# Opening of a two-layer encoder: two tiles turned by products with a diagonal of their roots, later tiles loaded into idle rows, and the last residual tile into a weight slot

## The chip, the cores and the metric

The kernel runs on one core of a Trainium2 chip. The metric is the device time of one execution in microseconds (us); lower is better. The core has a matrix engine (PE, with its weight loads PEld), a vector engine (DVE), a scalar engine (ACT), a general engine (POOL) and a queue engine (SP) that issues most transfers. Each engine takes its instructions in order; semaphores tie them together.

## The reference

Two groups of tokens (256 and 512) go through a trunk of width 1024 with two layers. Cut to what matters here:

```python
def rms_norm(x, g):
    return x * rsqrt(mean(x * x, axis=-1) + 1e-6) * g

for i in range(2):
    h = rms_norm(x, norm_mix_pre[i])
    m = window_gqa_sink(h, ...) if i == 0 else diff_attention(h, ...)   # each: qkv = h @ w_in, softmax, o @ w_o
    x = x + rms_norm(m, norm_mix_post[i])
    h = rms_norm(x, norm_ffn_pre[i])
    x = x + rms_norm(swiglu(h, w_gate_up, w_down), norm_ffn_post[i])
```

All is float32, and the products have to be nearly that exact.

## The kernel before

The 768 tokens are six tiles `t` of 128 rows. A tile is normalised row by row, turned (128 columns of it at a time, so that features lie on partitions) and split into a rounded high part `hhi` and a rest `hlo` (`split`, L364 on ACT and L365 on DVE); weights are split in the same way into `whi` and `wlo` (`two_parts`, L273 and L274). Each product of float32 accuracy is then three products `hi*hi`, `hi*lo`, `lo*hi` (L376 to L378).

The opening is what lies ahead of the first attention: for each tile, `scaled(row_rstd(x))` makes `y_pre` (square and row sum on ACT L427, plus epsilon on ACT L420, power -1/2 on POOL L421, times root and norm weight `gpre` on DVE L431); `transposes` turns it by eight PE transposes into two PSUM banks `tp_h` and splits each bank in one piece of 512 columns per engine. The key and value product of a tile, `pkva` (24 products, from four weight pieces `wa[0..3]`, two blocks `k` of 128 features each), needs all eight blocks of the tile. `a_fill` lists the order of the products: `pkva` of tiles 0, 1, 2, then the query product `pqa` of the first half, then `pkva` 3, 4, 5. `enter` and `entered` normalise tile `t + 2` while tile `t` is being multiplied. The order of the instructions on each engine is chosen by a scheduler within the constraints `issue_after`.

A tile `x` lies in one of two slots of the pool `xpool`; raw weights lie in two slots `wraw`. At the end of the second layer the down projection writes rows `y[t]` (`yf` in the profile); `finish` and `last_tile` add the residual tile `x`, which is read back from DRAM (`xd`), and store the sum (`ys`). The last residual tile, of tile 5, is loaded by `begin(5)` into an `xpool` slot, the one that tile 3 holds before. The rows `o[t]` (six tiles of 128x1024, name `oa`) take the attention output of the first layer; nothing is written to them in the opening.

Of the kernel before, what the change touches and what calls it, by code (L numbers as in the profile page):

```python
# [9 lines left out]
F32 = mybir.dt.float32  # L10
F32R = mybir.dt.float32r
BF16 = mybir.dt.bfloat16
AF = mybir.ActivationFunctionType
# [4 lines left out]
P = 128  # L18
# [70 lines left out]
def trunk(  # L89
# [18 lines left out]
    rope_b,  # L108
    yp,
# [166 lines left out]
    def prepare(upto):  # L276

        while state["split"] < min(upto, len(units), state["cap"] or len(units)):
# [35 lines left out]
            with ExitStack() as after:  # L314
                if state["after"] is not None:
                    after.enter_context(tc.issue_after(state["after"].ins))
                if 4 <= i < 8:
                    after.enter_context(tc.issue_after(state["rstd"].ins))
                    after.enter_context(tc.issue_after(state["scaled"].ins))
                if 4 <= i < N_PLAIN_A:  # L320
                    nc.gpsimd.dma_start(out=hi[:, :n], in_=raw_src[r][0])
                    state["raw_lo"] = nc.vector.tensor_tensor(
                        out=lo[:, :n], in0=src[:, :n], in1=hi[:, :n].bitcast(F32), op=ALU.subtract)
                else:
                    two_parts(hi[:, :n], lo[:, :n], src[:, :n])
# [365 lines left out]
    def mixer_a(gains, first_steps, o):  # L691
        with ExitStack() as st:
# [25 lines left out]
            def straight(i, t):  # L718
# [6 lines left out]
                def end():  # L725
# [5 lines left out]
                    rope(t1, t2, kr, pm[:, 256:].rearrange("p (n d) -> p n d", d=HD), 2, t)  # L731
# [412 lines left out]
    def ffn(layer, later, comb, cpool, cstack, ostack, gains):  # L1144
# [193 lines left out]
        with ExitStack() as st:  # L1338
# [144 lines left out]
            if not final:  # L1483
# [84 lines left out]
    head = ctx.enter_context(ExitStack())  # L1568
    first = head.enter_context(tc.tile_pool(name="first", bufs=1))
    xs_sb = [load_x(0, 0)]  # L1570
    g_in = gain(g_pre[0], "gpre", "0")
    fetch(2)
    xs_sb.append(load_x(0, 1))
    fetch(4)
    xs_sb.append(load_x(0, 2))
    small_inputs()
    xs_sb.append(load_x(0, 3))
    y_in = {}

    def enter(t):  # L1580
        x = xs_sb[t]
        y_in[t] = new_y(f"pre0_{t}")
        scaled(y_in[t], x, row_rstd(x, y_in[t], f"pre0_{t}"), g_in)

    def entered(t):
# [8 lines left out]
    enter(0)  # L1594
    with tc.issue_after(state["rstd"].ins), tc.issue_after(state["scaled"].ins):
        prepare(2)
    for s in transposes(y_in.pop(0), 0, "h0_0"):
        s()
    with tc.issue_after(state["hi"].ins), tc.issue_after(state["lo"].ins):
        enter(1)  # L1600
    with tc.issue_after(state["scaled"].ins), tc.issue_after(state["rstd"].ins):
        prepare(4)
    head.close()
    with tc.issue_after(state["raw_hi"].ins), tc.issue_after(state["raw_lo"].ins):
        small_tables()
        enter(2)
    ready = {t - 1: [lambda t=t: entered(t)] for t in range(1, NT)}

# [4 lines left out]

    def gains(i):
# [3 lines left out]
    o, ostack = rows("oa")  # L1618
# [8 lines left out]
def _layout(inp):  # L1627
# [51 lines left out]
    out["rope_b"] = c(np.stack([np.tile(rows(np.concatenate(p, axis=1)), (2, 1)) for p in ((cs, cs), (-sn, sn))]))  # L1679
    return out  # L1680
# [21 lines left out]
```

## Time and profile before

| | |
|---|---|
| time, median of 3 runs (lowest to highest) | 1643.13 us (1639.62 to 1646.32) |
| the profiled execution: its time, its span | 1638.01 us, 1636.2 us |
| PE busy in the span | 1607.4 us (98%) |
| DVE, ACT, POOL busy | 1201.5 us (73%), 942.5 us (58%), 169.3 us (10%) |
| first PE instruction | 8.04 us after the start |
| moved by DMA | 233.07 MB, mean 142 GB/s |

The profiled execution is the slowest core's own recording: its span runs from the first to the last instruction, and its time holds 1.8 us around it. Its time is 0.3% under the median of the runs. A busy share near 100% on PE means that a stage is bound there; where PE is idle, the row of its next instruction names what ended the wait.

### The profile page before, as it was taken

What the parts mean: (1) busy time and instruction counts of PE and PEld (TensorE: products, weight loads), DVE (VectorE), ACT (ScalarE), POOL (GpSimd) and SP (SyncE); (2) the same over time, 40 slices, a digit from 0 to 9 for tenths busy, and PEclk for the clock granted to TensorE, in tenths of its full rate; (3) what the DMA queues carried; (4) which work ended last, traced back from release to release, by engine and by line L of the source; (5) the groups of instructions that cost most, each with busy time, mean ns of one, the idle gap of its engine ahead of it and who ended that gap; (6) DMA issues with size and microseconds to landing.
All of it is one profiled execution on the core that took longest, in us unless ns stands there. A gap on an engine that the chain in (4) does not pass through costs nothing. (4 is left out here: it accounts for less than half of the span.)

```text
span 1636.2 us, 24435 instructions
## 1 busy us (share of the span) xinstructions
PE 1607.4 (98%) x9055; PEld 1489.5 (91%) x9055; DVE 1201.5 (73%) x2076; ACT 942.5 (58%) x1999; POOL 169.3 (10%) x261
## 2 busy tenths in 40 slices
PE   7999999999999999999999999999999999999998
PEld 7888878999999998888999999888999999998887
DVE  6778857887667755988585886857887667656986
ACT  6589976644444444556475666766644444444553
POOL 1121001000000000001220250421000000000010
PEclk9999999999999999999999999999999999999999
DMA  6532205443433247675432332505453432337664
GB/s 214 174 99 71 95 15 177 170 170 112 145 111 117 102 143 249 225 266 189 140 109 67 98 82 80 153 1 170 164 171 125 135 117 95 127 132 249 227 244 166
DMA packets 73384, 233.07 MB, mean 142 GB/s; under 512 B 9073, under 2 KB 17457, under 8 KB 73009
## 3 DMA queue, kind: packets, MB, share of 16 engines
q1 hardware_dynamic: 55008, 178.82, 32.1%
q0 software_dynamic: 18112, 52.44, 10.6%
q8 instruction: 71, 1.16, 0.3%
q14 instruction: 49, 0.39, 0.1%
q10 hardware_dynamic: 144, 0.26, 0.0%
HBM read 171.71 MB, written 42.86 MB: 131 GB/s over the span
## 5 line engine op out<-in xcount | busy, mean ns | idle before, releaser
L274 DVE TENSOR_TENSOR wlo<-wraw,whi 128x1024 fp32r<-128x1024 f32 (+1 forms) x161 | 190.7, 1188 | 185.4 <-ACT whi L273 184.7
L273 ACT CAST whi<-wraw 128x1024 fp32r<-128x1024 f32 (+1 forms) x161 | 164.6, 1024 | 124.5 <-PE py L377 59.2
L376 PE MATMUL py<-hhi,whi 128*128 128x384 f32 x480 | 160.9, 335 | 0.7 <-ACT whi L273 0.7
L377 PE MATMUL py<-hlo,whi 128*128 128x384 f32 x480 | 160.4, 334 | 0.0
L378 PE MATMUL py<-hhi,wlo 128*128 128x384 f32 x480 | 160.0, 334 | 0.0
L364 ACT CAST hhi<-araw 128x768 fp32r<-128x768 f32 (+1 forms) x74 | 57.6, 782 | 91.9 <-DMA araw<-act 89.5
L378 PE MATMUL pv<-whi,hlo 128*128 128x512 f32 (+1 forms) x240 | 92.2, 384 | 0.4 <-DVE hlo L365 0.4
L376 PE MATMUL pv<-whi,hhi 128*128 128x512 f32 (+1 forms) x240 | 92.4, 385 | 0.0
L377 PE MATMUL pv<-wlo,hhi 128*128 128x512 f32 (+1 forms) x240 | 92.3, 384 | 0.0
L376 PEld LDWEIGHTS py<-hhi,whi 128*128 128x128 f32 x480 | 90.1, 188 | 1.9 <-ACT whi L273 1.3
L377 PEld LDWEIGHTS py<-hlo,whi 128*128 128x128 f32 x480 | 90.1, 188 | 0.0
L378 PEld LDWEIGHTS py<-hhi,wlo 128*128 128x128 f32 x480 | 90.1, 188 | 0.0
L365 DVE TENSOR_TENSOR hlo<-araw,hhi 128x768 fp32r<-128x768 f32 (+1 forms) x74 | 65.2, 888 | 33.5 <-ACT hhi L364 33.3
L1228 POOL DMA_DIRECT2D act<-st x22 | 19.3, 877 | 631.5 <-DVE st L1227 601.3
L376 PE MATMUL po<-whi,hhi 128*128 128x512 f32 x192 | 78.5, 409 | 0.0
L376 PE MATMUL px<-hhi,whi 128*128 128x384 f32 x224 | 75.6, 337 | 1.7 <-ACT sv L1171 1.7
L1025 ACT ACTIVATE be<-bsc,bmx 128x512 f32<-128x512 f32 (+1 forms) x96 | 58.7, 614 | 29.7 <-DVE bmx L1023 29.2
L377 PE MATMUL po<-wlo,hhi 128*128 128x512 f32 x192 | 75.2, 392 | 0.0
L378 PE MATMUL po<-whi,hlo 128*128 128x512 f32 x192 | 75.2, 392 | 0.0
L377 PE MATMUL px<-hlo,whi 128*128 128x384 f32 x224 | 75.0, 335 | 0.0
L378 PE MATMUL px<-hhi,wlo 128*128 128x384 f32 x224 | 74.9, 334 | 0.0
L1023 DVE TENSOR_REDUCE bmx<-bsc 128x1 f32<-128x512 f32 (+1 forms) x96 | 55.2, 593 | 11.6 <-PE bsc L1019 11.3
(318 smaller groups left out, 4915.9 us busy)
## 6 DMA issues: line engine op xcount, KB each, us to landing
wraw<-in_wgu SPq DMA_DIRECT2D x60, 512.0 KB, 4.4
act<-st POOLq DMA_DIRECT2D x22, 1344.0 KB, 6.6
araw<-act SPq DMA_DIRECT2D x70, 384.0 KB, 3.9
y_wraw<-in_wgu SPq DMA_DIRECT2D x40, 512.0 KB, 4.0
wraw<-in_wd SPq DMA_DIRECT2D x40, 512.0 KB, 3.8
xd<-x SPq DMA_DIRECT2D x18, 512.0 KB, 2.9
x<-xd SPq DMA_DIRECT2D x18, 512.0 KB, 4.3
wraw<-in_wo SPq DMA_DIRECT2D x16, 512.0 KB, 3.5
```

The costliest lines, as they stand in the source:

```text
L273: state["raw_hi"] = nc.scalar.copy(out=hi, in_=src)
L274: state["raw_lo"] = nc.vector.tensor_tensor(out=lo, in0=src, in1=hi.bitcast(F32), op=ALU.subtract)
L364: state["hi"] = nc.scalar.copy(out=hi, in_=src)
L365: state["lo"] = nc.vector.tensor_tensor(out=lo, in0=src, in1=hi.bitcast(F32), op=ALU.subtract)
L376: nc.tensor.matmul(out, ah, bh, start=start and i == 0, stop=False, skip_group_check=more)
L377: nc.tensor.matmul(out, ah, bl, start=False, stop=False, skip_group_check=more)
L378: state["mm"] = nc.tensor.matmul(out, al, bh, start=False, stop=stop and i == last, skip_group_check=more)
L1023: nc.vector.tensor_reduce(out=mx, in_=s, axis=AX.X, op=ALU.max, negate=True)
L1025: nc.scalar.activation(out=e[:, :n * P], in_=s, func=AF.Exp, bias=mx, accum_out=den[:, c:c + 1])
L1228: nc.gpsimd.dma_start(out=at_hand[c // 4][:, :, c // 2 % 2], in_=out.pop(c // 2))
```

## The change

In the opening:

- Tile 0 comes in two halves of 512 columns, each squared on its own. A small input `g_col` holds the first norm weight as a column (feature `p` of block `k` at row `p`, column `k`).
- Tiles 0 and 1 are no longer scaled on DVE. The root of each row is put on a diagonal (`diag`, identity times root), and eight float32 products `x_block^T * diag` turn and scale in one. The norm weight is then a scale per partition in the split: ACT writes `hhi = g * v`, DVE writes `hlo = g * v - hhi`, both for one block of 128 columns at a time, so eight pieces on each engine and tile instead of two. Weight pieces 0 to 3 are split between these pieces; the first in two halves.
- Tiles 2 to 5 land in the idle rows `oa` early, all six loads standing ahead of the query weights on SP; `gpre` is loaded after the first weight pieces. Tiles 2 to 5 are normalised as before, but the squares of tile `t + 2` stand behind the split of tile `t`, and the scaling of tile `t + 1` behind that of tile `t`.
- The rotation of the keys on DVE stands behind the last scaled tile.

At the end, the residual tile of tile 5 lands in a slot of the raw weights (`wraw`), and its load stands ahead of the last tiles' work.

```diff
-    xs_sb = [load_x(0, 0)]
-    g_in = gain(g_pre[0], "gpre", "0")
+    o, ostack = rows("oa")
+    x0 = xpool.tile([P, D], F32, tag="x", name="x0_0")
+    for cols in halves_of:
+        nc.sync.dma_start(out=x0[:, cols], in_=x_at[0][0][:, cols])
+    nc.sync.dma_start(out=g_at, in_=g_col)
     fetch(2)
     xs_sb.append(load_x(0, 1))
     fetch(4)
-    xs_sb.append(load_x(0, 2))
-    small_inputs()
-    xs_sb.append(load_x(0, 3))
+    g_in = gain(g_pre[0], "gpre", "0")
+    for t in range(2, NT):
+        nc.sync.dma_start(out=o[t], in_=x_at[0][t])
+        xs_sb.append(o[t])
+        if t == 2:
+            small_inputs()
...
+    def diagonal(t, r):
+        diag = early.tile([P, P], F32, tag="diag", name=f"diag{t}", bufs=1)
+        state["scaled"] = nc.vector.tensor_scalar(out=diag, in0=ident, scalar1=r, scalar2=None, op0=ALU.mult)
...
+    def turn_first(t, x, diag):
...
+                nc.tensor.matmul(tp[:, j * P:(j + 1) * P], x[:, k * P:(k + 1) * P], diag, start=True, stop=True)
...
+        def part(k):
+            v = tps[k // 4][:, k % 4 * P:k % 4 * P + P]
+            h1, l1 = htile(t, k)
+            state["hi"] = nc.scalar.activation(out=h1, in_=v, func=AF.Copy, scale=g_at[:, k:k + 1])
+            state["lo"] = nc.vector.scalar_tensor_tensor(
+                out=l1, in0=v, scalar=g_at[:, k:k + 1], in1=h1.bitcast(F32), op0=ALU.mult, op1=ALU.subtract)
...
     def entered(t):
-        for s in transposes(y_in.pop(t), t, f"h0_{t}"):
-            s()
-        if t + 2 < NT:
-            if t + 3 < NT:
-                xs_sb.append(load_x(0, t + 3))
-            with tc.issue_after(state["hi"].ins), tc.issue_after(state["lo"].ins):
-                enter(t + 2)
+        if t == 1:
+            with behind("mm"):
+                part = turn_first(1, xs_sb[1], diag_1)
+            for k in range(KT):
+                with behind("hi", "lo"):
+                    part(k)
+            squares(2)
+        else:
+            for s in transposes(y_in.pop(t), t, f"h0_{t}"):
+                s()
+        if t + 1 < NT:
+            scale_in(t + 1)
...
+        if t + 2 < NT:
+            squares(t + 2)
...
+            x_of[5] = wpool.tile([P, 1024], F32, tag="wraw", name=f"x{sub}_5", bufs=RAW["w"])
+            load(x_of[5], x_at[sub][5])
...
                 if k == 0:
                     stage(4, 1)
-                    begin(5)
```

Where it moves instructions: first ACT around tiles 1 and 2. A name's first digit is the tile, `tp_h0_1_0` is the first bank of tile 1, `va0` the copy of tile 0's values out of `pkva0`. Before:

```order
L427 ACTIVATE y_pre0_2_219,ss_pre0_2_220<-x0_2_151 128x1024 [waits DMAHW7_49]
L364 CAST hhi0_110<-tp_h0_1_0_253 128x4x128 [waits PE_49]
L420 ACTIVATE rstd_pre0_2_222<-ss_pre0_2_220,eps_sb_103 128x1 [waits Activation_49]
L364 CAST hhi0_110<-tp_h0_1_1_260 128x4x128 [waits PE_49]
L727 COPY va0_288<-pkva0_240 128x256 [waits PE_49]
```

And now:

```order
L1627 ACTIVATE hhi0_110<-tp_h0_1_0_258,g_at_149 128x128 [waits PE_49]
L1627 ACTIVATE hhi0_110<-tp_h0_1_0_258,g_at_149 128x128 [waits DVE_49]
L730 COPY va0_318<-pkva0_245 128x256 [waits PE_49]
L1627 ACTIVATE hhi0_110<-tp_h0_1_0_258,g_at_149 128x128 [waits DVE_49] x2
L1627 ACTIVATE hhi0_110<-tp_h0_1_1_263,g_at_149 128x128
L1627 ACTIVATE hhi0_110<-tp_h0_1_1_263,g_at_149 128x128 [waits DVE_49] x3
L430 ACTIVATE y_pre0_2_284,ss_pre0_2_285<-oa2_139 128x1024 [waits DMAHW1_49]
L730 COPY va1_378<-pkva1_332 128x256 [waits PE_49,Activation_49]
L423 ACTIVATE rstd_pre0_2_287<-ss_pre0_2_285,eps_sb_103 128x1 [waits Activation_49]
```

The squares of tile 2 stood ahead of tile 1's split and now stand behind all of it, and the root of tile 2 behind the copy `va1`, which waits for the last product of tile 1. Each piece of `hhi` but the first of a bank waits for DVE: the semaphore's value is that of the `hlo` piece of the block before it, so the two engines take turns within a bank. Tile 0's pieces wait in the same way, with the splits of weight pieces 1 to 3 and the squares of tile 1 between them.

Second, PE from tile 1's product to tile 2's. Before, tile 2 is turned two products into `pkva1`:

```order
L376 MATMUL pkva1_302<-whi0_168,hhi0_110 128x384 [waits Activation_49]
L377 MATMUL pkva1_302<-wlo0_169,hhi0_110 128x384
L469 MATMUL tp_h0_2_0_312<-ident_81,y_pre0_2_219 128x128 [waits DVE_49]
L469 MATMUL tp_h0_2_0_312<-ident_81,y_pre0_2_219 128x128 x3
L469 MATMUL tp_h0_2_1_319<-ident_81,y_pre0_2_219 128x128 x4
L378 MATMUL pkva1_302<-whi0_168,hlo0_112 128x384 [waits DVE_49]
```

And now after the last product of `pkva1`, and right ahead of `pkva2`, which reads it:

```order
L381 MATMUL pkva1_332<-whi3_231,hlo0_112 128x384 [waits DVE_49]
L472 MATMUL tp_h0_2_0_342<-ident_81,y_pre0_2_284 128x128 [waits DVE_49]
L472 MATMUL tp_h0_2_0_342<-ident_81,y_pre0_2_284 128x128 x3
L472 MATMUL tp_h0_2_1_349<-ident_81,y_pre0_2_284 128x128 x4
L379 MATMUL pkva2_390<-whi0_193,hhi0_110 128x384 [waits Activation_49]
L380 MATMUL pkva2_390<-wlo0_194,hhi0_110 128x384
L381 MATMUL pkva2_390<-whi0_193,hlo0_112 128x384 [waits DVE_49]
```

Between the two products PE's order now holds nothing but the transposes of tile 2.

Third, SP at the end. Before, the load of the last residual tile stands behind a store and waits for a transfer:

```order
L247 DMA x3_3_15944<-xd2_3_129 128x1024 [waits DMAHW1_49,DMAHW0_49]
L247 DMA x3_4_16023<-xd2_4_130 128x1024 [waits DMAHW4_49]
L548 DMA ys<-x3_3_15944 128x1024 [waits DVE_49]
L247 DMA x3_5_16088<-xd2_5_131 128x1024 [waits DMAHW2_49]
L548 DMA ys<-x3_4_16023 128x1024 [waits DVE_49]
```

And now ahead of both stores, with no wait:

```order
L248 DMA x3_3_15973<-xd2_3_129 128x1024 [waits DMAHW3_49,DMAHW2_49]
L248 DMA x3_4_16052<-xd2_4_130 128x1024 [waits DMAHW6_49]
L248 DMA x3_5_16098<-xd2_5_131 128x1024
L551 DMA ys<-x3_3_15973 128x1024 [waits DVE_49]
L551 DMA ys<-x3_4_16052 128x1024 [waits DVE_49]
```

From the fourth key and value product to the end of the second layer's down projection, the order on all engines is what it was.

More of the change, by code (lines that the diff above doesn't have):

```diff
@@ L108, in trunk @@
     rope_b,
+    g_col,
     yp,
@@ L324, in prepare @@
                 else:
-                    two_parts(hi[:, :n], lo[:, :n], src[:, :n])
+                    for j in range(0, n, HALF if i == 0 else n):
+                        c = slice(j, j + HALF if i == 0 else n)
+                        two_parts(hi[:, c], lo[:, c], src[:, c])
             if kind == "t14" and units[i - 2][0] == "plain":
@@ L730, in end @@
                     kr, t1, t2 = (own[:, i] for i in range(3))
-                    rope(t1, t2, kr, pm[:, 256:].rearrange("p (n d) -> p n d", d=HD), 2, t)
+                    with tc.issue_after(state["scaled"].ins):
+                        rope(t1, t2, kr, pm[:, 256:].rearrange("p (n d) -> p n d", d=HD), 2, t)
                     if t == 0:
@@ new lines, in trunk, with norm_first @@
+    fetch(2)
+    xs_sb.append(load_x(0, 1))
+    fetch(4)
+    g_in = gain(g_pre[0], "gpre", "0")
[4 more added lines that the diff above has]
+            small_inputs()
+    y_in = {}
+    def norm_first(t, x):
+        ss = small.tile([P, 2], F32, tag="sso", name=f"ss_pre0_{t}")
+        junk = new_y(f"pre0_{t}")
+        cols = halves_of if t == 0 else [slice(0, D)]
+        for j, c in enumerate(cols):
+            nc.scalar.activation(
+                out=junk[:, c], in_=x[:, c], func=AF.Square, scale=D ** -0.5, accum_out=ss[:, j:j + 1])
+            if j == 0 and t == 0:
+                nc.scalar.activation(out=ss[:, 0:1], in_=ss[:, 0:1], func=AF.Identity, bias=eps_sb[:, 0:1])
+        return rstd(ss[:, 1:2], ss[:, 0:1], f"pre0_{t}") if t == 0 else rstd(ss[:, 0:1], eps_sb[:, 0:1], f"pre0_{t}")
@@ new lines, in diagonal @@
+    def diagonal(t, r):
+        diag = early.tile([P, P], F32, tag="diag", name=f"diag{t}", bufs=1)
+        state["scaled"] = nc.vector.tensor_scalar(out=diag, in0=ident, scalar1=r, scalar2=None, op0=ALU.mult)
+        return diag
+    def turn_first(t, x, diag):
+        tps = []
+        for b in range(2):
+            tp = bank(f"tp_h0_{t}_{b}")
+            for j in range(4):
+                k = 4 * b + j
+                nc.tensor.matmul(tp[:, j * P:(j + 1) * P], x[:, k * P:(k + 1) * P], diag, start=True, stop=True)
+            tps.append(tp)
+        def part(k):
[4 more added lines that the diff above has]
+                out=l1, in0=v, scalar=g_at[:, k:k + 1], in1=h1.bitcast(F32), op0=ALU.mult, op1=ALU.subtract)
+        return part
@@ new lines, in behind, with two @@
+    def behind(*names):
+        stack = ExitStack()
+        for n in names:
+            stack.enter_context(tc.issue_after(state[n].ins))
+        return stack
+    def two(part, k):
+        for j in (k, k + 1):
+            part(j)
+    r0 = norm_first(0, x0)
+    part = turn_first(0, x0, diagonal(0, r0))
+    with behind("rstd", "scaled"):
+        prepare(1)
+    with behind("raw_hi", "raw_lo"):
+        two(part, 0)
+    with behind("hi", "lo"):
+        prepare(2)
+    with behind("raw_hi", "raw_lo"):
+        two(part, 2)
@@ new lines, in trunk, with squares @@
+    with behind("hi", "lo"):
+        prepare(3)
+    with behind("raw_hi"):
+        r1 = norm_first(1, xs_sb[1])
+    with behind("rstd", "raw_lo"):
+        two(part, 4)
+    with behind("rstd", "hi", "lo"):
+        diag_1 = diagonal(1, r1)
+        prepare(4)
+    with behind("raw_hi", "raw_lo"):
+        two(part, 6)
+    head.close()
+    rs = {}
+    def squares(t):
+        y_in[t] = new_y(f"pre0_{t}")
+        with behind("hi", "rstd"):
+            rs[t] = row_rstd(xs_sb[t], y_in[t], f"pre0_{t}")
@@ new lines, in scale_in, with entered @@
+    def scale_in(t):
+        with behind("lo"):
+            scaled(y_in[t], xs_sb[t], rs.pop(t), g_in)
+    def entered(t):
+        if t == 1:
+            with behind("mm"):
+                part = turn_first(1, xs_sb[1], diag_1)
+            for k in range(KT):
+                with behind("hi", "lo"):
+                    part(k)
[5 more added lines that the diff above has]
+            scale_in(t + 1)
+        if t == 1:
+            with behind("scaled"):
+                small_tables()
+        if t + 2 < NT:
+            squares(t + 2)
@@ L1614, in gains @@
+    ready = {t - 1: [lambda t=t: entered(t)] for t in range(1, NT)}
     def gains(i):
```

32 lines of the change are left out of this document (6 added, 26 removed).

## The prediction

> **What bounds the kernel now.** I read the busy shares first, then the stretches around the two edited places, then the instructions there in order of time.
>
> ```profile
> PE 1607.4 (98%) x9055; PEld 1489.5 (91%) x9055; DVE 1201.5 (73%) x2076; ACT 942.5 (58%) x1999; POOL 169.3 (10%) x261
> 8.00:20.00 12.00, 11.63 (x54) 10.31 (x55) 9.33 (x16) 8.84 (x18) 1.78 (x3) 1.00 1.02 373
> 20.00:48.00 28.00, 28.00 (x179) 27.65 (x178) 19.10 (x49) 15.24 (x43) 3.85 (x7) 1.00 0.30 98
> 48.00:80.00 32.00, 28.97 (x183) 27.00 (x182) 26.29 (x83) 19.96 (x63) 6.54 (x12) 1.00 0.63 209
> ```
>
> The kernel is bound by PE. In the stretches (second column the length, third PE's busy time) PE works almost without a gap from 8 to 48 us; so whatever delays PE's first work, or opens a gap before 48 us, moves everything behind it. In the opening:
>
> ```profile
> 4.13 1.06 ACT L427 ACTIVATE y_pre<-x 128x1024 f32<-128x1024 f32 x1 [1.90 <-DMA x<-in_xp]
> 5.68 0.56 POOL L421 TENSOR_TENSOR rstd_pre<-rstd_pre,mhalf 128x1 f32<-128x1 f32 x1 [3.55 <-ACT rstd_pre L420]
> 6.70 1.28 DVE L431 SCALAR_TENSOR_TENSOR y_pre<-x,rstd_pre,gpre 128x1024 f32<-128x1024 f32 x1 [4.73 <-DMA gpre<-in_g_pre]
> 7.63 0.83 ACT L273 CAST whi<-wraw 128x768 fp32r<-128x768 f32 x1 [2.03 <-DMA wraw<-in_wa]
> 8.04 1.97 PE L469 MATMUL tp_h<-ident,y_pre 128*128 128x128 f32 x8 [8.04 <-DVE y_pre L431]
> 8.50 0.96 DVE L274 TENSOR_TENSOR wlo<-wraw,whi 128x768 fp32r<-128x768 f32 x1 [0.52 <-ACT whi L273]
> 9.49 1.14 ACT L364 CAST hhi<-tp_h 128x512 fp32r<-128x512 f32 x2
> 10.12 0.69 PE L376 MATMUL pkva<-whi,hhi 128*128 128x384 f32 x1
> 10.50 1.28 DVE L365 TENSOR_TENSOR hlo<-tp_h,hhi 128x512 fp32r<-128x512 f32 x2
> 12.36 0.52 PE L378 MATMUL pkva<-whi,hlo 128*128 128x384 f32 x1
> 12.68 0.52 PE L376 MATMUL pkva<-whi,hhi 128*128 128x384 f32 x1
> 16.82 0.34 PE L376 MATMUL pkva<-whi,hhi 128*128 128x384 f32 x1
> 16.99 0.34 PE L377 MATMUL pkva<-wlo,hhi 128*128 128x384 f32 x1
> 18.49 1.09 PE L469 MATMUL tp_h<-ident,y_pre 128*128 128x128 f32 x8
> 23.27 0.33 PE L376 MATMUL pkva<-whi,hhi 128*128 128x384 f32 x1
> 28.67 0.33 PE L376 MATMUL pqa<-hhi,whi 128*128 128x384 f32 x1
> 46.32 0.40 PE L791 MATMUL sc<-ka,qa 128*128 128x256 f32 x2
> ```
>
> The first transposes (8.04) end a chain: tile 0 lands (4.13), its root is ready at 5.68 + 0.56 = 6.24, the norm weight lands only at 6.70, the scaling takes 1.28. Products follow each other every 0.32 us at first (12.36 to 12.68) and every 0.17 us later (16.82 to 16.99): PE begins at half its rate. 23.27 is the first product of `pkva2`, with tile 2 turned long before, at 18.49; 28.67 the first of `pqa0`; 46.32 the first score. These are the marks I compare with.
>
> **The opening, part by part.** Prices of the new kinds of work, from the same operations in other stages (in the first two rows: busy us in all, mean ns of one):
>
> ```profile
> L1048 ACT ACTIVATE hhi<-tp_o,subl 128x128 fp32r<-128x128 f32 x6 | 2.2, 373 | 0.5 <-PE tp_o L1045 0.5
> L1049 DVE SCALAR_TENSOR_TENSOR hlo<-tp_o,subl,hhi 128x128 fp32r<-128x128 f32 x6 | 2.1, 346 | 1.0 <-ACT hhi L1048 1.0
> 839.70 1.06 PE L1074 MATMUL pob<-vb,aT 128*128 128x128 f32 x8
> 840.51 0.42 PE L376 MATMUL pkb<-hhi,whi 128*128 128x384 f32 x1
> 1.67 0.30 DVE L130 CAST ident_r<-ident 128x128 fp32r<-128x128 f32 x1 [0.74 <-POOL ident masks.py:199]
> 23.46 0.37 ACT L727 COPY va<-pkva 128x256 f32<-128x256 f32 x1 [1.59 <-PE pkva L378]
> ```
>
> The same scaled split of one 128-column block takes 0.37 us on ACT and 0.35 on DVE. Four float32 products of 128 columns (`pob`) are eight records and take 840.51 - 839.70 = 0.81 us, so 0.20 each; at half rate 0.40, while a transpose costs half of that (eight in 0.85, 18.49 to 19.34).
>
> 1. *Start.* The halves land by about 4 us: their bytes are the first of what lands at 4.13 now. I put the first square at 3.9, the second 0.9 later (an estimate: half of 1.06, the reading of its sum, the epsilon), the roots at 6.5 (one POOL power of 0.56 as before), diagonal 0.30: PE starts at 6.8, between 6.2 (second half squared right at 4.13) and 7.2. That is 1.2 us earlier than 8.04; the norm weight no longer delays it.
> 2. *Eight products* at half rate: bank 0 is whole after 1.6 us and 0.3 of latency, at 8.7; PE is free for `pkva0` at 10.0, as before (10.12). The gain of step 1 is spent.
> 3. *Tile 0's pieces.* A hand-over takes 0.04 us (`whi` ends at 8.46, `wlo` starts at 8.50), so a block costs 0.37 + 0.04 + 0.35 + 0.04 = 0.80 us in turns, eight of them 6.4; now the whole tile is split by 11.78 (10.50 + 1.28), 1.7 us after its banks. In order from 8.7, with the weight splits (0.83 and 0.96) and the squares of tile 1 (1.06, and 0.1 until its sum is read) between the pieces as the order has them: second piece by 10.25, `whi1` 9.8 to 10.6, `wlo1` to 11.6, pieces three and four to 12.7, `whi2` 12.2 to 13.0, squares to 14.1, `wlo2` to 14.0, pieces five and six 14.3 to 15.9, `whi3` to 16.2, `wlo3` to 17.2, pieces seven and eight to 18.3. PE follows, turns tile 1 at 16.1 to 17.7, and ends `pkva0` at 18.8.
> 4. *Tile 1's pieces* have nothing beside them: eight turns of 0.80 from 17.8, less 0.35 at the change of bank and plus 0.1 for the copy `va0`; the last `hhi` ends at 23.3, the last `hlo` at 23.65. `pkva1` needs 24 x 0.17 = 4.2 us and is stretched to 18.8 to 24.2.
> 5. *The hole.* Then tile 2's root waits for the copy `va1` (0.37), in front of it on ACT, and that for `pkva1`: copy from 24.2, root 24.5 to 24.8, POOL to 25.4, scaling 1.28 to 26.7, transposes from 26.7, the first `hhi` (half of the 1.14 at 9.49) 27.4 to 28.0. `pkva2` starts at 28.0 against 23.27. PE idles 2.5 us, then 0.4 and, before the first `hlo`, 0.35.
> 6. *Beyond.* `pkva2` with the transposes in it took 5.4 us (23.27 to 28.67) and takes 5.8 with that last wait, so `pqa0` starts at 33.8, 5.1 later. From there the pieces are the old ones, and by the score (46.32) the same adding up gives +5.0. The same adding up, with the old order and rows, puts the old score at 46.16.
>
> Bounds: with hand-overs of 0.09 each way and pieces of 0.42 and 0.40 the delay is 6.1; with pieces at 0.2 us, below the 0.30 of the plain 128-column cast at 1.67, still 2.9, since the hole of step 5 does not depend on them. I take 5.0, from the rows of the very operation.
>
> The loads cost nothing. `gpre` (512 KB) moves behind the first weights and is needed at 25.4; tiles 2 to 5 land by about 18, in a stretch where DMA is full anyway (1.02 of its share, 8 to 20 us), and are needed from 23.2 on. They stand ahead of the first query weights on SP, whose split is now due at about 32; gone, that cover would cost a wait before `pqa0`. The 32-byte rows of `g_col` are needed at 8.7.
>
> **The end.**
>
> ```profile
> 1611.62 0.86 SPq L247 DMA_DIRECT2D x<-xd  x2
> 1627.83 3.76 DMA x<-xd
> 1630.59 0.55 POOL L421 TENSOR_TENSOR rstd_last<-rstd_last,mhalf 128x1 f32<-128x1 f32 x1 [3.39 <-ACT rstd_last L420]
> 1631.71 1.41 DVE L568 SCALAR_TENSOR_TENSOR x<-yf,rstd_last,x 128x512 f32<-128x512 f32 x2 [1.12 <-DMA x<-xd]
> ```
>
> The store of tile 3's sum frees the slot, the load of tile 5 follows it (1627.83, 3.76 us), and the last addition starts at 1631.71 on its landing. The new load is issued behind the other two (1611.62) and lands ten microseconds before it is needed; next late is the root, ready at 1630.59 + 0.55 = 1631.14. The addition starts at about 1631.17: a gain of 0.54. Its second half now waits for the end of the first, 0.12 later than at the present spacing of 0.66. Net -0.4.
>
> **Sum.** +5.0 - 0.4 = +4.6 us. The profiled execution would be 1638.0 + 4.6 = 1642.6. The median of the runs is 5.1 us above that execution, so the forecast for the time is 1643.1 + 4.6 = 1647.7 us, 0.3% slower, within the 0.5% that I take as what a measurement of this kernel tells from no change.
>
> **Rivals.**
>
> ```profile
> 49.45 0.41 PE L376 MATMUL pqa<-hhi,whi 128*128 128x384 f32 x1 [0.66 <-DMA whi<-in_waf]
> 73.72 0.63 PE L832 MATMUL tpe<-ident,y_e 128*128 128x128 f32 x4 [1.98 <-DVE y_e L814]
> 74.53 0.34 PE L376 MATMUL pqa<-hhi,whi 128*128 128x384 f32 x1
> 74.71 0.33 PE L377 MATMUL pqa<-hlo,whi 128*128 128x384 f32 x1
> ```
>
> *The delay is swallowed, and the end's gain is left (not slower).* PE waits 32.0 - 28.97 = 3.0 us between 48 and 80, and more later (all idle time is 1636.2 - 1607.4 = 28.8, of which 8.0 ahead of the start). If these waits ended on something that does not move with PE, a late opening would fill them; from 5.0 us of such waits on it costs nothing: 1642.7. Against it: the waits end on DVE's softmax (73.72) and on a weight load that PE's own products release (49.45), which move along.
>
> *Cheap pieces.* If pieces go at 0.2 us, +2.9 - 0.4: 1645.6. For it: neighbours on one engine do overlap; against: the two engines hand over each time, and L1048 and L1049 are that operation.
>
> *PE falls back to half rate in the hole.* The first stretch at half rate lasted from 8.04 to about 15. Another 7 us of it in and behind the hole would put the score another 2.4 later: 1650.1. Against it: after the pause of 1.98 us ahead of 73.72, products still come every 0.18 (74.53 to 74.71). [...]
>
> **Numbers.** Forecast 0.53, swallowed 0.20, cheap pieces 0.15, half rate 0.10, the rest other. The runs of the kernel spread by 3 us either way, so the range reaches from 1640.5 (below the swallowed case) to 1652 (above the half rate case). Faster by over 0.5% (under 1634.9) only noise on the swallowed case: 0.03; slower by over 0.5% (over 1651.3) the half rate case or noise on the forecast: 0.11; within: 0.86.
>
> **What would show it.** PE's first product near 6.8 (step 1), `pkva0` from about 10 (2), `hhi` and `hlo` pieces in strict turns about 0.8 us apart (3, 4), PE idle some 2.5 us ahead of tile 2's transposes, released by the scaling on DVE (5), the first score near 51 (6), and the last addition released by POOL, not by a DMA (end). A score near 46 would refute the opening's sum; a score near 51 with a span no longer than before would say that the delay was swallowed.

## The result, and the profile after

The changed kernel takes 1649.1 us (median of 7 runs, 1647.1 to 1656.7), the kernel before in the same sessions 1641.7 us. The ratio is 1.005 (95% interval 1.0037 to 1.0063), so it is 0.4 to 0.6% slower: 7.4 us between the medians and 8 by the ratio, where 4.6 were forecast. Measured again (below), the ratio is 1.0042 (1.0030 to 1.0054). The profiled execution has a time of 1649.13 us and a span of 1647.4 us. Ratios leave out runs in a slower state; among the variants below these are one of 2974.6 us (tile 2 ahead) and one of 5703.5 us (warm start, early loads and both pauses).

The marks of the opening, in the changed kernel. First PE's rows in order of time (the lines have moved: L376 to L378 are now L379 to L381, L469 is L472, L791 is L795):

```profile
6.63 3.40 PE L1621 MATMUL tp_h<-diag,x 128*128 128x128 f32 x16 [6.63 <-DVE diag L1612]
9.78 0.42 PE L379 MATMUL pkva<-whi,hhi 128*128 128x384 f32 x1
14.67 0.44 PE L379 MATMUL pkva<-whi,hhi 128*128 128x384 f32 x1 [1.52 <-ACT hhi L1627]
16.13 3.48 PE L1621 MATMUL tp_h<-diag,x 128*128 128x128 f32 x16
28.40 1.09 PE L472 MATMUL tp_h<-ident,y_pre 128*128 128x128 f32 x8 [2.68 <-DVE y_pre L434]
29.73 0.52 PE L379 MATMUL pkva<-whi,hhi 128*128 128x384 f32 x1 [0.24 <-ACT hhi L367]
30.05 0.52 PE L380 MATMUL pkva<-wlo,hhi 128*128 128x384 f32 x1
36.95 0.33 PE L379 MATMUL pqa<-hhi,whi 128*128 128x384 f32 x1
54.43 0.40 PE L795 MATMUL sc<-ka,qa 128*128 128x256 f32 x2
```

PE starts at 6.63, `pkva0` at 9.78; tile 2 is turned at 28.40 after a wait of 2.68 us on its scaling; the first score stands at 54.43, 8.1 us behind that of before (46.32). Then the pieces on ACT, whose bracket says what the engine waited for, and on DVE the scaling of tile 2:

```profile
8.74 0.37 ACT L1627 ACTIVATE hhi<-tp_h,g_at 128x128 fp32r<-128x128 f32 x1 [0.39 <-PE tp_h L1621]
9.53 0.37 ACT L1627 ACTIVATE hhi<-tp_h,g_at 128x128 fp32r<-128x128 f32 x1 [0.42 <-DVE hlo L1628]
18.72 0.37 ACT L1627 ACTIVATE hhi<-tp_h,g_at 128x128 fp32r<-128x128 f32 x1 [0.42 <-DVE hlo L1628]
20.80 0.37 ACT L730 COPY va<-pkva 128x256 f32<-128x256 f32 x1 [1.71 <-PE pkva L381]
21.07 0.37 ACT L1627 ACTIVATE hhi<-tp_h,g_at 128x128 fp32r<-128x128 f32 x1
23.69 0.37 ACT L1627 ACTIVATE hhi<-tp_h,g_at 128x128 fp32r<-128x128 f32 x1 [0.42 <-DVE hlo L1628]
24.48 0.37 ACT L1627 ACTIVATE hhi<-tp_h,g_at 128x128 fp32r<-128x128 f32 x1 [0.42 <-DVE hlo L1628]
24.88 0.35 DVE L1628 SCALAR_TENSOR_TENSOR hlo<-tp_h,g_at,hhi 128x128 fp32r<-128x128 f32 x1 [0.43 <-ACT hhi L1627]
27.06 1.28 DVE L434 SCALAR_TENSOR_TENSOR y_pre<-oa,rstd_pre,gpre 128x1024 f32<-128x1024 f32 x1 [1.83 <-POOL rstd_pre L424]
```

The pieces come in turns of 0.79 us (8.74 to 9.53, 23.69 to 24.48), each `hhi` released by the `hlo` before it, as steps 3 and 4 had it. At 20.80 the copy `va0` stands in the row and makes ACT wait 1.71 us for `pkva0`.

Two rows of the forecast look wrong at once: eight products with the diagonal took 3.48 us at 16.13, where four take 0.81 at full rate elsewhere, and `pkva2`'s products at 29.73 follow each other every 0.32 us. PE was at half rate there. In stretches of 3.41 us (second column the length, third PE's busy time; after the engines the granted clock, the DMA share and GB/s):

```profile
12.89:16.30 3.41, 1.89 (x10) 1.24 (x10) 2.00 (x5) 2.96 (x8) 1.22 (x2) 1.00 0.69 247
16.31:19.72 3.41, 3.41 (x17) 3.41 (x17) 2.12 (x5) 1.19 (x4) 0.00 (x0) 0.50 1.04 397
26.55:29.96 3.41, 1.32 (x9) 1.08 (x10) 2.53 (x9) 2.02 (x6) 1.41 (x2) 1.00 0.02 5
29.96:33.37 3.41, 3.41 (x11) 3.00 (x11) 3.41 (x8) 1.93 (x6) 0.91 (x1) 0.50 0.01 2
```

The clock was granted in full from 9.48 to 16.31, by half from 16.31 to 19.72 and from 29.96 to 33.37, each time for one stretch of 3.41 us (these five times lie whole multiples of 3.41 us apart, 3.41 to 10.24; the other boundaries are counted on from them), and each time right behind a stretch in which PE had been busy little more than half or less (1.89 and 1.32 of 3.41).

Behind the score nothing of it is given back, and not all of this execution's 11 us are the opening's: starts of the same PE instructions show +8.1 at the score, +7.8 at 230 us, +9.8 at 395 and +11.3 at 1216, and the kernel of the first experiment below, which has the old opening, shows -0.1, +0.3, +3.2 and +2.9 at the same places. So 3 us of the difference are scatter: the profiled execution of before was a short one.

The end:

```profile
1641.90 0.55 POOL L424 TENSOR_TENSOR rstd_last<-rstd_last,mhalf 128x1 f32<-128x1 f32 x1 [3.38 <-ACT rstd_last L423]
1642.48 1.42 DVE L571 SCALAR_TENSOR_TENSOR x<-yf,rstd_last,x 128x512 f32<-128x512 f32 x2 [0.59 <-POOL rstd_last L424]
```

The last addition is released by POOL, 0.58 us after its root began; before it was 1.12, on a DMA.

### The profile page after: what moved, and what is told of

The parts are those of the page before. It is cut to its first block, busy times and chain, and to the rows that moved or that the text cites. A ratio compares the mean times of both kernels' runs of the same rounds, so it can differ in the third digit from the quotient of the medians.

```text
span 1647.4 us, 24502 instructions
## 1 busy us (share of the span) xinstructions
PE 1613.1 (98%) x9071; PEld 1492.9 (91%) x9071; DVE 1202.8 (73%) x2089; ACT 945.2 (57%) x2015; POOL 165.9 (10%) x261
## 5 line engine op out<-in xcount | busy, mean ns | idle before, releaser
L275 DVE TENSOR_TENSOR wlo<-wraw,whi 128x1024 fp32r<-128x1024 f32 (+3 forms) x162 | 190.9, 1182 | 186.4 <-ACT whi L274 185.7
L274 ACT CAST whi<-wraw 128x1024 fp32r<-128x1024 f32 (+3 forms) x162 | 164.6, 1019 | 124.9 <-PE py L380 56.1
L379 PE MATMUL py<-hhi,whi 128*128 128x384 f32 x480 | 161.1, 336 | 3.3 <-ACT u L1189 1.7
L381 PE MATMUL py<-hhi,wlo 128*128 128x384 f32 x480 | 160.1, 334 | 0.0
L379 PEld LDWEIGHTS py<-hhi,whi 128*128 128x128 f32 x480 | 90.1, 188 | 5.2 <-ACT u L1189 2.4
L379 PE MATMUL pv<-whi,hhi 128*128 128x512 f32 (+1 forms) x240 | 92.4, 385 | 0.4 <-DVE yf L1388 0.4
L381 PE MATMUL pv<-whi,hlo 128*128 128x512 f32 (+1 forms) x240 | 92.3, 384 | 0.4 <-DVE hlo L368 0.4
L381 PEld LDWEIGHTS py<-hhi,wlo 128*128 128x128 f32 x480 | 90.1, 188 | 0.0
L379 PE MATMUL po<-whi,hhi 128*128 128x512 f32 x192 | 78.6, 409 | 0.0
L379 PE MATMUL px<-hhi,whi 128*128 128x384 f32 x224 | 75.4, 337 | 2.0 <-ACT sv L1175 2.0
L381 PE MATMUL po<-whi,hlo 128*128 128x512 f32 x192 | 75.2, 392 | 0.0
L381 PE MATMUL px<-hhi,wlo 128*128 128x384 f32 x224 | 74.9, 334 | 0.0
```

The costliest lines, as they stand in the source:

```text
L274: state["raw_hi"] = nc.scalar.copy(out=hi, in_=src)
L275: state["raw_lo"] = nc.vector.tensor_tensor(out=lo, in0=src, in1=hi.bitcast(F32), op=ALU.subtract)
L379: nc.tensor.matmul(out, ah, bh, start=start and i == 0, stop=False, skip_group_check=more)
L381: state["mm"] = nc.tensor.matmul(out, al, bh, start=False, stop=stop and i == last, skip_group_check=more)
```

## The experiments

All ratios are against the kernel before, in runs of its own on the same chip; "score" is the start of PE's first score (before: 46.32; changed: 54.43).

**The end alone.**

```diff
+            x_of[5] = wpool.tile([P, 1024], F32, tag="wraw", name=f"x{sub}_5", bufs=RAW["w"])
+            load(x_of[5], x_at[sub][5])
...
-                    begin(5)
```

> The kernel before, with the change at the end alone: the residual tile of tile 5 lands in a weight slot, its load ahead of the last tiles' work. Prediction's step (end): the last addition is released by POOL's root instead of the landing of x, 0.54 us earlier, second half 0.12 later: 0.4 us faster than the kernel before (ratio 0.9997, so not to be told from 1 by the time; the row's releaser decides). Rival: the load takes a weight slot that the last weight pieces want, PE waits for a late weight and the time is 1 us or more longer.

Ratio 0.9993 (0.998 to 1.0005), score 46.23.

```profile
1634.05 1.41 DVE L568 SCALAR_TENSOR_TENSOR x<-yf,rstd_last,x 128x512 f32<-128x512 f32 x2 [0.59 <-POOL rstd_last L421]
```

Counted from PE's last product (1631.65 here, 1628.78 before) the addition starts 2.40 us later instead of 2.93: 0.53 us gained, as the step had it, too little for the time to show. The second half follows 0.67 us behind the first as before, so the 0.12 that I took off weren't lost.

**Blocks in alternating banks.**

```diff
-                k = 4 * b + j
+                k = 2 * j + b
...
-            v = tps[k // 4][:, k % 4 * P:k % 4 * P + P]
+            v = tps[k % 2][:, k // 2 * P:k // 2 * P + P]
```

> The changed kernel, with the blocks of tiles 0 and 1 turned into the two banks in alternation (block k into bank k mod 2), so that ACT's next piece never lies in the bank that DVE is reading. Theory of the turns (steps 3 and 4): tile 1's pieces follow each other every 0.4 us instead of every 0.8, the last hhi ends near 21.5 instead of 24.85, and everything behind it, tile 2's transposes and the first score, comes some 3.4 us earlier (score near 51 instead of 54.4); time 3 to 4 us under the changed kernel. Rival: the pieces are 0.8 us apart because ACT and DVE need the time anyway, or because the products of PE release them; then nothing moves.

Ratio 1.0022 (1.0011 to 1.0032), score 48.05: 6.4 us earlier than in the changed kernel, where 3.4 were expected. ACT's pieces now go in pairs 0.79 us apart, two pieces per turn:

```profile
17.19 0.63 ACT L1627 ACTIVATE hhi<-tp_h,g_at 128x128 fp32r<-128x128 f32 x2 [0.53 <-PE tp_h L1621]
17.98 0.63 ACT L1627 ACTIVATE hhi<-tp_h,g_at 128x128 fp32r<-128x128 f32 x2 [0.16 <-DVE hlo L1628]
```

So the turns were due to the shared bank: the order makes each piece wait for the other engine's piece in the same bank. The other 3 us I put down to the clock (the two stretches at half rate cost 2.95 in the account below): PE's wait ahead of tile 1's turn is 0.67 us here instead of 1.52, and no stretch of the opening is at half rate in this trace. It is at half rate further on, behind a wait that the kernel before has too (the weights of the first attention, from DVE, at 73.72, there 1.98 us long):

```profile
76.95 0.63 PE L836 MATMUL tpe<-ident,y_e 128*128 128x128 f32 x4 [3.27 <-DVE y_e L818]
...
74.42:77.83 3.41, 0.88 (x7) 0.91 (x8) 3.40 (x14) 2.16 (x7) 0.04 (x1) 1.00 0.42 154
77.84:81.25 3.41, 3.41 (x14) 3.18 (x12) 3.19 (x11) 2.97 (x10) 1.13 (x2) 0.50 0.17 60
```

**Tile 2 ahead.**

```diff
+            squares(2)
             for k in range(KT):
                 with behind("hi", "lo"):
                     part(k)
-            squares(2)
+                if k == 3:
+                    scale_in(2)
...
-        if t + 1 < NT:
+        if 1 < t < NT - 1:
             scale_in(t + 1)
```

> The changed kernel, with tile 2's squares ahead of tile 1's pieces and its scaling in the middle of them; the pieces stay in turns. Theory of the hole (step 5): tile 2's transposes no longer wait for pkva1 (the copy va1, the root, the scaling): they run inside pkva1, the idle time of 2.7 us ahead of them is gone. Tile 1's pieces come 1.1 to 1.3 us later. By the same adding up as in the prediction the first score comes 2.1 us earlier (52.3). If the half rate behind the hole came from the idle time, that goes too, for 1.6 us more: score near 50.7. Rival: the delay sits in the pieces alone, and moving tile 2's work between them costs what it saves: score at 54 or later.

Ratio 1.0024 (1.0009 to 1.0039), score 49.33: 5.1 us earlier than in the changed kernel, 2.1 and 1.6 of the clock were expected. Tile 2 is turned 5.3 us earlier, and PE waits 0.40 for it instead of 2.68:

```profile
23.14 1.09 PE L472 MATMUL tp_h<-ident,y_pre 128*128 128x128 f32 x8 [0.40 <-DVE y_pre L434]
```

No stretch of this opening is at half rate. At tile 1's turn that isn't the edit's doing: PE waits 1.53 us ahead of it (13.21 to 14.74), as in the changed kernel, but a boundary between two stretches of 3.41 us, at 14.02 in this trace, cuts this wait, and the stretches on its two sides hold 2.60 and 2.70 us of work. So about 1.5 of the 5.1 us, the price of that stretch in step 4 below, look like luck.

**PE kept busy in the pauses.** In `straight`, which lists a tile's products:

```diff
+                def keep(n):
+                    w = bank(f"keep{t}")
+                    with tc.issue_after(state["mm"].ins):
+                        for _ in range(n):
+                            state["mm"] = nc.tensor.matmul(w[:, :P], ident, ident, start=True, stop=True)
+                if t == 0:
+                    steps = steps[:4] + [lambda: keep(6)] + steps[4:]
+                if t == 1:
+                    steps = steps + [lambda: keep(12)]
...
-                p = 4 if i == 0 else 3
+                p = {0: 5, 1: 9}.get(i, 3)
```

> The changed kernel, with products of the identity with itself that nobody reads, only to keep PE busy: 6 behind the fourth block of pkva0, where PE waits 1.5 us, and 12 behind the last product of pkva1, ahead of tile 2's transposes, where it waits 2.7 us (0.20 us each at full rate). Nothing else of the order is meant to move. Theory of the clock: the granted rate of a window of 3.4 us follows from how busy PE was in the window before; with the pauses filled the two windows at half rate (16.3 to 19.7 and 30.0 to 33.4 in the changed kernel) are at full rate, tile 1's products take 1.6 us instead of 3.2, pkva2's start no 1.6 more: first score near 51.3 instead of 54.4, as the prediction's sum without the clock had it, time about 3 us under the changed kernel, mean clock .999. Rival: the half rate costs nothing, since PE waits for the pieces anyway, or falls for another reason: score and time as in the changed kernel, or later by what the added products take.

```profile
24.44 2.84 PE L732 MATMUL keep<-ident 128*128 128x128 f32 x24
27.29 1.09 PE L472 MATMUL tp_h<-ident,y_pre 128*128 128x128 f32 x8
52.06 0.40 PE L806 MATMUL sc<-ka,qa 128*128 128x256 f32 x2
...
24.48:27.89 3.41, 3.40 (x31) 3.22 (x30) 1.95 (x7) 2.11 (x7) 1.49 (x2) 1.00 0.00 2
27.90:31.31 3.41, 2.96 (x18) 2.40 (x17) 3.29 (x10) 2.96 (x8) 0.24 (x1) 1.00 0.01 2
...
80.18 0.63 PE L847 MATMUL tpe<-ident,y_e 128*128 128x128 f32 x4 [2.81 <-DVE y_e L829]
75.68:79.09 3.41, 1.70 (x11) 1.37 (x9) 3.19 (x6) 2.29 (x8) 0.10 (x1) 1.00 0.33 125
79.10:82.51 3.41, 2.33 (x16) 2.21 (x17) 3.23 (x15) 3.20 (x10) 1.17 (x2) 1.00 0.52 185
```

With products that nobody reads in the pauses the clock stays whole in the opening, and the score stands at 52.06: 2.4 us earlier with more work on PE, 5.7 later than before. That is the size of turns and hole without the clock; the sum had 5.0. The time, however, did not fall: ratio 1.0052 (1.0040 to 1.0064). In its trace the 2.4 us are given back by 230 us (+8.2 there against +7.8 in the changed kernel). They go at waits: PE, which comes earlier, waits 2.81 us for DVE ahead of 80.18 (1.97 in the changed kernel) and 0.76 us for ACT ahead of 210.88, where the changed kernel doesn't wait. Why DVE and ACT aren't earlier by as much isn't settled; the added products take two turns in the rotation of eight banks, so later stages aren't the same.

**The changed kernel once more**, unchanged.

> The changed kernel once more, unchanged. In the first profile two windows of 3.41 us at half rate lay in its opening, and the mean clock of its runs lay between .995 and .998. Theory of the free-running window: where the windows fall against the pauses differs from execution to execution, so this profile shows none, one or two of them in the opening, and the first score at about 52, 53 or 54.4 accordingly (each costs 0.8 to 1.7 us); without any it would be at 51 to 52, as with the added products (52.06). Over the runs, one thousandth less of mean clock (one more window) goes with 1 to 2 us more span. Rival: the half rate is tied to the program's pauses; then the windows lie at the same places again and the score is at 54.4.

Ratio 1.0042 (1.0030 to 1.0054), score 54.03. There are two stretches at half rate in the opening again (and one each at 81.1 and 309.8, behind later pauses), but not the same two: the turn of tile 1 is at full rate, and the two lie one behind the other at the hole:

```profile
12.87:16.28 3.41, 2.10 (x10) 1.37 (x10) 1.93 (x5) 2.96 (x7) 1.22 (x2) 1.00 0.67 229
23.11:26.52 3.41, 1.43 (x6) 0.78 (x5) 1.13 (x3) 3.20 (x8) 0.56 (x1) 1.00 0.41 165
26.52:29.93 3.41, 2.71 (x11) 2.26 (x12) 2.58 (x12) 1.43 (x5) 0.94 (x1) 0.50 0.03 7
...
27.22 1.97 PE L472 MATMUL tp_h<-ident,y_pre 128*128 128x128 f32 x8 [2.68 <-DVE y_pre L434]
```

The boundaries lie within 0.03 us of where they lay in the first profile. But up to 16.28 PE was busy 2.10 us of its stretch instead of 1.89, and the rate stayed full; so tile 2's transposes come 1.2 us earlier and fall into the half rate themselves (1.97 instead of 1.09 us). The wait ahead of them is 2.68 us in both executions; by these figures the two profiles differ in 0.2 us of work in one stretch ahead of the half rate, and in which stretches are slowed. That the boundaries lie elsewhere in other executions, as expected, this pair doesn't show; the boundary at 14.02 in the run with tile 2 ahead, against 12.89 here, does. The runs of the two kernels by mean clock (the profiler's, three digits; one thousandth less is about one window at half rate), mean time and number of runs of all sessions:

| mean clock | before | changed |
|---|---|---|
| .999 | 1641.0 (24) | none |
| .998 | 1642.7 (45) | 1648.1 (5) |
| .997 | 1643.8 (28) | 1649.9 (3) |
| .996 | 1644.8 (2) | 1651.2 (2) |
| .995 | none | 1654.4 (2) |

One run of the kernel before, with a recorded clock of .948 and 1641.6 us, is not in the table.

At equal clock the changed kernel is 5.4 to 6.4 us slower; and its clock is lower, .9969 on average against .9979. The one thousandth is an estimate: half of 3.41 us in 1640.

**Banks and tile 2 together.**

> The changed kernel with both undone: blocks in alternating banks, and tile 2's squares and scaling ahead of and within tile 1's pieces. Alone the banks put the first score at 48.05 and the order put it at 49.33 (before: 46.32, changed: 54.43). Theory (turns and hole are all of the delay): together the first score is near 46.6 by the same adding up as in the prediction, so the opening is worth nothing either way, and the time is within 0.1% of the kernel before. Rival: something else of the opening holds it back, such as the first weight piece, which lands later, or the loads; then the score stays near 48.

Ratio 1.0004 (0.9994 to 1.0015), score 46.68. Both edits together take back 7.8 of the 8.1 us: turns, hole and the half rate that they bring are all of the delay but 0.4 us. The late first weight piece and the loads hold back no more than that.

**PE warmed before its first work**: 15 products of the identity in the old opening, from 1.69 us, with the end of the first experiment.

```diff
             tp = bank(f"tp_{name}_{b}")
+            if name == "h0_0" and b == 0:
+                for _ in range(15):
+                    nc.tensor.matmul(tp[:, :P], ident, ident, start=True, stop=True)
```

> The kernel before with the change at the end, and with 15 products of the identity with itself at the very start of PE, which waits there until 8.04 us; nobody reads them. Theory of the clock: PE gets its full rate before tile 0 is turned instead of at 15.2 us, the transposes take 0.9 instead of 2.0 us, pkva0's first products come every 0.17 instead of 0.32 us, and the first score comes 2.0 us earlier by adding up (near 44.3); time 2 us under the kernel before, 0.4 of which is the end's. Rival: the opening is bound by the pieces of the weights as they land, so a faster PE only waits for them, and the score stays near 46.

Ratio 1.0003 (0.9992 to 1.0014), score 49.81: a miss. The rate rose at 7.6 us (products from 11.51 follow each other every 0.17 us), but the edit also moved the load of tile 3 on SP, behind a query weight and a table of the rotation; ACT waited for it and then PE, which fell to half rate at 28.1:

```profile
22.96 1.06 ACT L427 ACTIVATE y_pre<-x 128x1024 f32<-128x1024 f32 x1 [3.31 <-DMA x<-in_xs]
...
26.87 1.06 PE L472 MATMUL tp_h<-ident,y_pre 128*128 128x128 f32 x8 [2.02 <-DVE y_pre L431]
```

**The same warm start with all of the above**: alternating banks, tile 2 ahead, 11 products at the start.

> The changed kernel with alternating banks, tile 2 moved ahead, and 11 such products at PE's start. Tile 0's eight products with the diagonal then run at full rate: 1.6 us instead of 3.2. By adding up the first score is 1.7 us earlier than without them (near 45), and the time about 1 us under the kernel before. Rival: tile 0's pieces wait for the weight splits between them on ACT and DVE, and the score is near 46.6 as without.

Ratio 1.0007 (0.9998 to 1.0016), score 45.70, 0.6 us earlier than before, and no gain in the time: the trace has stretches at half rate at 74.2 and 302.9 us, behind pauses that the kernel before has as well (there 1.98 and 0.72 us long, here 1.98 and 2.54).

**Those two pauses filled.** Seven products ahead of the fourth bank of `tpe`, eight ahead of the second half of the first `px`, the rest as in the first experiment (what was meant; where the products ran is below).

```diff
                 tp = bank(f"tpe{g}_{t}_{j}")
+                if (g, t, j) == (0, 0, 3):
+                    with tc.issue_after(state["mm"].ins):
+                        for _ in range(7):
+                            nc.tensor.matmul(tp[:, :P], ident, ident, start=True, stop=True)
...
+            if c == 0 and layer == 0:
+                keep = bank("keepf")
+                with tc.issue_after(state["mm"].ins), tc.high_priority():
+                    for _ in range(8):
+                        nc.tensor.matmul(keep[:, :P], ident, ident, start=True, stop=True)
             mul(X, c, "px", "a12", unit, 1, True)
```

> The kernel before with the change at the end, and with PE's two longest later pauses filled by products that nobody reads: 7 ahead of the fourth bank of transposed weights of the first attention (its pause of 2.0 us ahead of 73.7) and 8 ahead of the second half of the first gate product (pause of 0.7 to 2.5 us near 299). In the traces so far a window of 3.41 us in which PE was busy under half was followed by one at half rate, and these two pauses had such windows in seven of the ten profiles. Theory of the windows: no window at half rate remains but the last one, mean clock .999 in most runs instead of .9978 on average, time 1 to 2 us under the kernel before. Rival: PE waits there for DVE and ACT anyway, so the half rate behind the pauses costs nothing, or the added products delay what follows: time as before or longer.

```profile
70.47 1.72 PE L832 MATMUL tpe<-ident 128*128 128x128 f32 x14
73.57 0.66 PE L836 MATMUL tpe<-ident,y_e 128*128 128x128 f32 x4 [1.37 <-DVE y_e L814]
...
287.17 1.95 PE L1182 MATMUL keepf<-ident 128*128 128x128 f32 x16
300.78 0.44 PE L376 MATMUL px<-hhi,whi 128*128 128x384 f32 x1 [1.55 <-ACT sv L1175]
...
69.57:72.98 3.41, 2.63 (x22) 2.44 (x20) 3.35 (x10) 2.13 (x8) 0.00 (x0) 1.00 0.34 106
```

The clock did as it should: .999 or more in 10 of 12 runs. The time went the other way, ratio 1.0024 (1.0015 to 1.0032). But the edit did only half of what it was meant to do. The seven products stand in the first pause, of which 1.37 us are left. The eight ran from 287.17, some 10 us ahead of the second pause, where PE waited for nothing, and 1.55 us of that pause are left (300.78). The starts are 1.1 us behind those of the kernel before ahead of these eight products and 2.9 behind them; so they explain 1.8 of the 3.9 us. What the rest is isn't settled, and what it is worth to fill the second pause this run doesn't say.

**Warm start with early loads**, so that tile 3 isn't late (the old opening, tiles 2 to 5 loaded into `oa`, 15 products, the end).

> The kernel before with the change at the end, 15 products ahead of PE's first work as in the run with the warm start, and tiles 2 to 5 loaded early into the idle rows, as in the change, so that tile 3 can't land late as it did there (ACT waited 3.3 us for it). Theory of the clock: full rate from about 7.6 us; by adding up the first score is at 44.4 instead of 46.3 and the time 2 us under the kernel before. Rival: with PE at full rate the opening is bound by tile 2's scaling on DVE (it ended at 18.3 in the run with the warm start, and PE waited 1.05 us for it): the score is not before 45.5 and the gain under 1 us.

Ratio 0.9994 (0.9985 to 1.0004), score 45.04, 1.3 us earlier than before where 1.9 were added up: between theory and rival. By 77 us it is given back: 0.4 us to the same pause, 2.42 us long here instead of 1.98, and the rest to a stretch at half rate behind it:

```profile
69.59:73.00 3.41, 0.98 (x7) 0.69 (x6) 3.38 (x10) 2.16 (x9) 0.00 (x0) 1.00 0.35 115
73.00:76.41 3.41, 3.41 (x14) 3.31 (x13) 2.63 (x10) 3.34 (x9) 1.09 (x2) 0.50 0.31 118
```

**Warm start, early loads and both pauses filled.**

> Warm start, early loads, the end, and the two filled pauses together. If each is worth what its theory says: 3 to 4 us under the kernel before (ratio 0.998), the fastest of all so far. Rival: none of it reaches the end, since later waits give it back; ratio 1.000.

Ratio 1.0015 (1.0004 to 1.0026), score 45.03. Here too the eight products ran ahead of their pause, at 286.39, and cost 1.8 us; so this run doesn't price filled pauses either.

**Transposes in place of the warming products**, shown against the kernel of the warm start with early loads, which is otherwise unchanged.

```diff
-                for _ in range(15):
-                    nc.tensor.matmul(tp[:, :P], ident, ident, start=True, stop=True)
+                for _ in range(24):
+                    nc.tensor.transpose(tp[:, :P], ident, ident)
```

> The kernel of the warm start with early loads, with 24 transposes of the identity (0.25 us each at half rate, from 1.7 to about 7.7 us) in place of the 15 products. In the kernel before, PE got its full rate only at 15.18, though it was busy 93% of the window from 8.35 to 11.76 (half of it transposes), while in the changed kernel a window busy 84% with products (6.07 to 9.48) was enough. Theory: transposes don't count as work for the granted rate; then the rate rises only at 11.8 to 15.2 again and the score is at about 46. Rival: any busy window counts; then the rate rises by 8.5 us at the latest and the score is at 45.0 as with products.

Ratio 0.9991 (0.9975 to 1.0007), score 45.65. The theory fell: the rate rose at 5.36 us, with nothing but transposes on PE from 1.69 on. The two stretches from there on held nearly the same work:

```profile
5.36:8.77 3.41, 1.76 (x16) 1.52 (x15) 1.60 (x2) 1.20 (x4) 0.55 (x1) 1.00 1.00 373
8.78:12.19 3.41, 1.84 (x10) 1.28 (x9) 2.79 (x4) 3.38 (x7) 0.18 (x1) 1.00 1.02 409
12.19:15.60 3.41, 3.41 (x15) 3.28 (x14) 3.00 (x4) 2.61 (x5) 1.04 (x2) 0.50 0.89 285
```

The one with 1.76 us of work was followed by one at full rate, the one with 1.84 by one at half rate: in these two the profile's busy time doesn't decide it.

## Why the prediction was right or wrong, step by step

The direction was right, and the time lies in the range. The size was too small: 4.6 us forecast, 8 and 7 measured by the two ratios, and the case that I gave 0.10 is in the main the one that happened: 6.8 us at half rate where it had 7, and a score 3.1 us behind the sum where it had 2.4. But one of the two stretches lay ahead of the hole, at tile 1's turn, where I hadn't looked for it. That 1647.7 is only 1.4 us under the measured 1649.1 is luck in part: it started from 1643.1 us for the kernel before, which took 1641.7 in the same sessions.

1. *Start*: 6.63 against 6.8. Right.
2. *Eight products*: at half rate as forecast, bank 0 whole in time for the first piece at 8.74 (8.7), `pkva0` from 9.78 (10.0). Right. After them PE was at full rate already (9.48), 5.7 us earlier than in the kernel before, which it could not use, since it waited for the pieces.
3. *Tile 0's pieces*: turns of 0.79 us (0.80), tile 1 turned from 16.13 (16.1). Right, and the alternating banks show that the shared bank makes the turns.
4. *Tile 1's pieces*: first piece at 17.94 (17.8), last `hhi` ends at 24.85 against 23.3. The turns were right (as written, my terms add up to about 23.5; the change of bank saves 0.54 us in the trace, 21.86 to 22.11 instead of a turn, not 0.35); the copy `va0`, which I had put at 0.1, cost 1.6 (the next piece at 21.07 instead of 19.51), since `pkva0` ended 1.8 later. The cause is the eight products at 16.13: 3.48 us at half rate instead of 1.6.
5. *The hole*: from the last `hhi` to the transposes 3.55 us (3.4), PE idle for 2.68 (2.5). Right, and tile 2 moved ahead removes it.
6. *Beyond*: `pkva2` to `pqa0` 7.2 us (5.8). The 1.4 more are its first products at half rate. From `pqa0` to the score 17.5 as before (17.65).

So +8.1 at the score is 5.0 + 1.55 (step 4) + 0.15 (step 5) + 1.4 (step 6), and both large terms are the clock. With PE kept busy in the pauses the delay was 5.7, against 5.0 added up; at equal mean clock the whole kernel is 5.4 to 6.4 us slower.

*The step that failed* is the argument against the half rate. I held that a pause of 1.98 us in the trace had left the rate alone, and that a hole of 2.5 us would too; the second no run had shown. In the fourteen profiles PE's longest wait behind its first work was 3.27 us, and yet of the windows of 3.41 us at full rate every one of 15 in which PE was busy under 45% was followed by one at half rate, 3 of 14 between 45 and 56%, and none of some 250 between 56 and 90%. So in these traces the half rate came behind windows in which PE was busy for at most 56%, and in none of them had a pause filled the window. The boundaries of the windows don't follow the program: one lay at 14.02 in the run with tile 2 ahead, at 12.89 in the changed kernel, with the same order of PE's work up to there. The pause of 2.68 us that ended at 28.40 lay for 1.85 us in the window from 26.55, which held 1.32 us of work, and the half rate followed; it followed too behind the wait of 1.52 us ahead of 14.67, with smaller ones beside it (1.89 us of work). The pause of 2.81 us ahead of 80.18 in the run with PE kept busy was cut by a boundary at 79.09, which left 1.70 and 2.33 us of work in its two windows, and no half rate followed (the mean clock of this trace is .999, as in that of before). That one pause of 1.98 us was harmless proved nothing: the same wait, between 1.98 and 3.27 us long, was followed by a window at half rate in six other traces; at 1.98 us too, in the warm start with all of the above.

*The loads* cost nothing, as said: no wait of PE ahead of the score ends on a load. *Swallowed delay*: no; the same waits follow the delay, as argued. *Cheap pieces*: no, 0.37 and 0.35 us each, in turns.

*The end*: gained 0.53 (0.54) up to the addition. But in every kernel with the changed opening the stretch from the addition to the end of the span is 4.87 us instead of 4.49, so 0.38 is lost again. The traces show where: at the end of the program SP waits for the semaphores of the transfers one after another, 0.06 us apart. The last store lands 3.5 us after that addition began either way; its semaphore stands second of nine in this row in the kernels with the changed opening, with seven waits behind it, and eighth in the others, with one behind it. Six more waits are 0.37 us. My step for the end had no such term.

## What to carry to other kernels

Here two engines that read the same PSUM bank in small pieces, with an order that makes one wait for the other, went in turns of 0.79 us, the sum of their times (0.37 and 0.35 us, and the hand-overs); with the blocks in alternating banks two pieces went in 0.79 us. So put neighbouring blocks into different banks before cutting an operation into pieces. When a change opens a pause on the engine that bounds the kernel, price it twice: its own length, and, as a chance, a window of 3.41 us at half rate behind it (1.55 and 1.4 us for the two in the changed kernel's opening): in these traces one came behind every one of 15 windows in which PE was busy under 45% and behind 3 of 14 between 45 and 56%, and the program did not set where the boundaries fell (14.02 against 12.89). And when you fill a pause with idle work, look in the trace whether the work runs in the pause: eight products here ran 10 us ahead of theirs and were pure cost. Don't count a gain at a mark as a gain at the end: four variants here reached the first score 0.6 to 1.3 us earlier than before, and none was measurably faster.

## What the runs showed of the hardware that was not expected

- In these traces the granted clock changed in windows of 3.41 us (in the changed kernel at 9.48, 16.31, 19.72, 29.96 and 33.37) whose boundaries did not follow the program, and the number of windows at half rate differed between executions of one program: ahead of the end two in the changed kernel's first profile, four in its second. That goes with part of the scatter of its times (means of 1641.0 at .999 to 1643.8 at .997 in the kernel before), but at .999 alone they still reach from 1636.4 to 1643.9.
- The rate rose at 5.36 us in the run with transposes, where PE had work from 1.69. In the kernel before it rose only at 15.18, though PE was busy for 3.19 of the 3.41 us up to 11.76; why that window didn't count stays open, since in the changed kernel 2.85 us of work up to 9.48 were enough. Nor did 2.71 us of work at half rate bring the rate back at 29.93 in its second profile. That it was transposes in part doesn't explain it by these runs, since at 5.36 the rate rose behind transposes alone. (These times are those of the trace's first record of the full clock; ahead of it the clock column prints 1.00, though the products come at half rate.)
- A mean clock of .999 or more in 10 of 12 runs did not make the kernel faster: with idle products added it was 0.24% slower, of which the eight that missed their pause explain about half.
